# A float32 encoder block on one core: a fifth seven-product unit in ten FFN blocks, fourth sums added by the transfer, residual rows kept in DRAM

## The chip, the cores and the metric

The kernel runs on one core of a Trainium2 chip. The metric is the device time of one execution in microseconds (us), lower is better. Times of several runs are given by their median.

## The reference, cut to what matters

One layer of an encoder with 256 tokens, width 2048 and FFN width 5632, all in float32. Three token mixers (dilated windows, grouped-query attention, cross-attention into 256 memory tokens) are merged by gates; the change lies in what comes after:

```python
x = x + merged @ w_o                                  # residual add, 2048 -> 2048
hf = rms_norm(x, g_ffn) @ w_ffn_in                    # 2048 -> 2 x 5632
x = x + (silu(hf[..., :D_FF]) * hf[..., D_FF:]) @ w_ffn_out   # 5632 -> 2048
```

## The kernel before

**Products.** Every float32 product is made of three fp32r matmuls. A weight block `[128, 2 k-tiles, 512 columns]` (512 KB) is split into a high part `whi` (written by ACT, line 433) and a low part `wlo` (written by VectorE, line 443: the block less `whi`). The tokens' side is kept split in the same way. One product is `x_hi w_hi + x_hi w_lo + x_lo w_hi` for 128 tokens, 128 k and 512 columns, issued at line 79 in this order of terms.

**Blocks and units.** `pair()` computes two 512-column tiles for the two halves of the tokens (four PSUM banks) out of units of k. A plain unit (`D6`, `d6`: the two column tiles of k pair 6) takes eight products of two k-tiles each by two token halves. Units 0 to 3 are taken two and two (`doubles`) by a scheme with seven products for eight, named by the letters X, W, P, Y, Q, Z and H. It needs sums of weight blocks and of tokens: for one double, with blocks b11, b12, b21 and b22, `t = b11 + b12` for W, for P `t` with b22 added (line 576, in its place), for Q this `t` less b11 (line 578, in the place of b11) and for H `t` plus b21 (line 580, in the place of b21). The first sum, `t`, is made by a transfer: b12 is loaded, and a DMA of POOL's queue adds b11 to it (line 530). The others are VectorE additions of 1024 columns. The sums of tokens (`forms`) are made once in `token_sums` from the transposed tiles.

**Order.** The strings `STEPS_...` give the order of steps in a block: `l0` begins double 0 (loads and the accumulating transfer), `r0` loads its second half, `X0` is the product X of double 0, and a dot takes a step of the block before, whose last plain units (third string) run in the front of the next. TensorE's instructions and the loads of SP's queue are kept in the order written. On VectorE and ACT, the instructions that pass through `follow` (`whi`, `wlo`, the sums) keep their order among themselves; the others (the residual adds, the transposed copies) are placed by a scheduler, in a list that the engine then works off in order. Weight blocks are loaded ahead into eleven places (`raw`, `more`, `both`), each free again when the `whi` and `wlo` of its block are written. There are five pairs of `whi` and `wlo`, and `run(everything(), 4)` readies four units ahead.

**Stages.** `merging`, then `projecting` (the product with w_o in two `pair()` calls, residual add into the rows `x`, line 947), then `feeding`: eleven FFN blocks of 512 hidden columns in chunks of 4, 4 and 3, each chunk followed by two parts of the output product (`pairs`), whose result is scaled by a row factor and added to `x` on VectorE (line 1007); in the last chunk each piece of `x` is then stored to the output. The two tiles `x` lie in SBUF from `projecting` to the end.

Of the kernel before, what the change touches and what calls it, by code (L numbers as in the profile page):

```python
# [103 lines left out]
def encoder_block(ctx: ExitStack, tc: tile.TileContext, a: dict, out: bass.AP):  # L104
# [192 lines left out]

    def transposed(src, dst, g=None, lag=1, also=None):


        full = None
        for h in range(2):
            if h:
                yield lag
            tp = bank("tp", "tp")
            for k in range(2):
                for t in range(T):
                    nc.tensor.transpose(tp[:, k * S + t * P:k * S + (t + 1) * P],
                                        src[t][:, (2 * h + k) * P:(2 * h + k + 1) * P], ident)
            if g is None:  # L310
                d = dst(2 * h, 2)
                split(d[0], d[1], tp.rearrange("p (k s) -> p k s", s=S))
            else:
                for k in range(2):
                    d = dst(2 * h + k, 1)
                    split(d[0], d[1], tp[:, k * S:(k + 1) * S], g(2 * h + k))
            if also is not None:
                if full is None:
                    full = s4([P, 2, 4, P], "ffull")
                to, of = full[:, :, 2 * h:2 * h + 2], tp.rearrange("p (k t s) -> p k t s", t=T, s=P)  # L320
                if g is None:
                    nc.scalar.activation(to, of, AF.Copy)
                else:
                    for k in range(2):
                        nc.scalar.activation(to[:, k], of[:, k], AF.Copy, scale=g(2 * h + k))
        if also is not None:
            token_sums(full, also)

    def token_sums(full, to):


        raw = s4([P, 2, 4, P], "fraw")
# [40 lines left out]
    def hold(n, steps):  # L373
        yield n
        yield from steps
# [44 lines left out]
    def halves(*srcs, each=None):  # L420

        count[0] += 1
        pool, n = (more[0], 1) if more and count[0] % 5 == 0 else (wp, 4)
        hi = pool.tile([P, PK, NC], F32R, name="whi", bufs=n)
        lo = pool.tile([P, PK, NC], F32R, name="wlo", bufs=n)
        n = 0
        for v in srcs:
            v = v.unsqueeze(1) if len(v.shape) == 2 else v
            o = slice(n, n + v.shape[1])
            if each:  # L430
                low(0)
                each(n)
            nc.follow(nc.scalar.activation(hi[:, o], v, AF.Copy))  # L433
            due.append((lo[:, o], v, hi[:, o].bitcast(F32)))
            n += v.shape[1]
        return hi, lo
# [3 lines left out]
    def low(n):  # L440

        while len(due) > n:
            nc.follow(nc.vector.tensor_sub(*due.pop(0)))  # L443

    def pair(src, lhs, lists, done, doubles=(), forms=None, operand=None, fresh="", early=False, by_halves=False):

# [10 lines left out]
        nd, wholes = len(doubles), {c: sum(o[0] == c for o in order) for c in "dD"}  # L457
        left = {"Y": 2 * nd + 2 * wholes["d"], "X": 6 * nd, "V": 2 * nd + 2 * wholes["d"],
                "W": 4 * nd + 2 * wholes["D"], "Q": 2 * wholes["D"]}
        if not early:  # L460
            left["X"] += left.pop("V")
        ends = "YV" if early else "YX", "WQ"
        stops = {"X": [left["X"] - n * nd for n in (2, 4, 6)], "W": [left["W"] - 2 * nd]}
        ps, raws, seen, ended = {}, {}, {}, set()
# [76 lines left out]
        def phase_end(kind, hi):  # L541
            seen[kind] = seen.get(kind, 0) + 1
            if seen[kind] < nd:
                return
            with tc.high_priority():
# [13 lines left out]
                if kind == "Q":  # L559
                    new("Q")  # L560
                    wake("Q", hi)
                    nc.follow(nc.vector.tensor_sub(ps["Q"], raws["m5"], ps["X"]))

        def seventh(kind, m):
            of = {"X": "b11", "W": "t", "Y": "b21", "P": "t", "Z": "b22", "Q": "b11", "H": "b21"}[kind]
            bk = {"P": "X", "Q": "X", "H": ends[0][1], "Z": "W"}.get(kind, kind)
            needs = {"Y": "X", "P": "X", "Z": "P", "Q": "P", "H": "Q"}

            def ready():
                r = raws[m]  # L570
                raw = r[of]
                if kind in "PQH" and last_kind[0] == {"P": "W", "Q": "X", "H": "Y"}[kind] + str(m):
                    low(0)
                last_kind[0] = kind + str(m)
                if kind == "P":
                    nc.follow(nc.vector.tensor_add(raw, raw, r["b22"]))
                elif kind == "Q":
                    nc.follow(nc.vector.tensor_sub(raw, r["t"], raw))  # L578
# [3 lines left out]
                for n in {"Q": ["b11"], "Z": ["b22"], "H": ["t", "b21"]}.get(kind, ()):  # L582
                    release(r.pop(n))

                def products():
                    assert kind not in needs or seen.get(needs[kind], 0) == nd, (kind, seen)
                    assert kind != "Z" or seen["W"] == nd
                    for i in range(2):
# [3 lines left out]
                              "Z": lambda: forms(m, i, 2), "Q": lambda: forms(m, i, 3)}[kind]()  # L592
                        mul(bk, st, hi[:, i], lo[:, i])
                    phase_end(kind, hi)
# [4 lines left out]
        def step(o):  # L599
# [3 lines left out]
            if kind in "dD":  # L603
                return whole(n, "dD".index(kind))
            if kind in "lr":
                return lambda: (begin if kind == "l" else begin2)(n)
            return seventh(kind, n)
# [260 lines left out]
    home = lambda n: big if n == 3 else tail  # L868
    mT, x1T, x, room = {}, [], [], []
    ss1 = const.tile([P, T, 4], F32, name="ss1")  # L870
# [55 lines left out]
    def projecting():  # L926
# [8 lines left out]
        ended = []  # L935

        def root():
            yield 4
# [4 lines left out]
        for n in (0, 2):  # L943
            def add(c, r, n=n):
                xc = [x[t][:, (n + c) * NC:(n + c + 1) * NC] for t in range(T)]
                for t in range(T):
                    nc.vector.tensor_add(xc[t], r[t], xc[t])
                ended.append(n + c)
                last = len(ended) == 4

                def later():
# [7 lines left out]
                    if not x1T:  # L959
                        x1T.extend(s8([P, 2, 4, S], "x1T") for _ in range(4))  # L960
                        room.extend(form_room(3))
                    yield from transposed(xc, lambda k, m: (x1T[n + c][:, 0, k], x1T[n + c][:, 1, k]),
                                          lambda k: gT[:, 2, 4 * (n + c) + k:4 * (n + c) + k + 1], 2,
                                          also=room[2 + n + c] if n == 0 else None)
                start(urgent(later()))
# [3 lines left out]
    def store(t, o):  # L969
        nc.sync.dma_start(out=out[t * P:(t + 1) * P, o], in_=x[t][:, o])  # L970
        yield 1

    def feeding():
        for c0, c1 in ((0, 4), (4, 8), (8, KF // 4)):
# [3 lines left out]
            for n in range(c0, c1):  # L978
                av = []

                def hidden(c, v, av=av, n=n - c0, hT=hT):
# [8 lines left out]
                    def later():  # L990
# [5 lines left out]
                    start(urgent(later()))  # L996
                yield pair(lambda u, c, n=n: a["w_ffn"][n][2 * u + 1 - c], x1l, STEPS_FFN if n else STEPS_FFN0, hidden,
                           TWO, by_room(lambda: room[2:]))
            pairs = (STEPS_LAST, STEPS_LAST2) if last else (STEPS_FFN, STEPS_FFN)
            for n in (0, 2):  # L1000
                def output(c, r, n=n, last=last):
                    final = last and n == 2 and c == 0
                    w = NC // 2 if final else NC
                    for t in range(T):
                        for h in range(NC // w):
# [3 lines left out]
                                                           op0=ALU.mult, op1=ALU.add)  # L1009
                            if last:  # L1010
                                start(hold(1 if n else 4, store(t, o)))

# [93 lines left out]
```

## Time and profile before

| | us |
|---|---|
| three runs | 1359.69, 1359.86, 1361.61 |
| median | 1359.86 |
| the profiled execution | 1359.78 |
| its span | 1358.0 |

Between span and time of the profiled execution lie 1.78 us. The clock granted to TensorE was 1.00 throughout. The window from 581 to 700 us holds the end of `projecting` and the first FFN block, the one from 700 to 1281.85 the other ten FFN blocks with the output parts of the first two chunks and the beginning of the last, the one from 1281.85 to the end the last parts. In rows of the profile `mmX`, `mmY`, `mmW` and `mmQ` are the PSUM tiles of a block; a row of the chain of waits gives start, length, engine, tile, line and the number of instructions. A timeline's row gives start and length, and in brackets the idle time ahead of it and who ended that.

### The profile page before, as it was taken

The numbers are of one execution on the slowest core, as the hardware profiler recorded it, in microseconds if no ns is written. First come the engines' busy times: TensorE is split into PE (matmuls) and PEld (weight loads), VectorE is DVE, ScalarE is ACT, GpSimd is POOL, SyncE is SP. The second block draws the span as 40 slices with busy tenths as digits, with TensorE's granted clock in tenths as the row PEclk, the third lists the DMA queues.
The fourth block names the chain that finished last, engine by engine and source line by source line (L and its number), as shares of the span: only waits on it lengthen the run. The fifth ranks groups of instructions, "written<-read, shape, count | busy, mean of one in ns | idle before, by whom it ended". The sixth has DMA issues, their size and how long they took to land.

```text
span 1358.0 us, 17334 instructions
## 1 busy us (share of the span) xinstructions
PE 1351.8 (100%) x6176; PEld 1121.4 (83%) x6176; DVE 1157.1 (85%) x1412; ACT 856.4 (63%) x1112; POOL 53.1 (4%) x60
## 2 busy tenths in 40 slices
PE   9999999999999999999999999999999999999998
PEld 8888888888888888888888888888888888888887
DVE  6878877778879869778899998988999889989997
ACT  7877656656656656657676666555666655566664
POOL 0010000000000000000000000000000000000000
PEclk9999999999999999999999999999999999999999
DMA  9976445556787584785577766688666787666872
GB/s 365 348 231 208 153 146 174 165 171 215 231 264 219 188 293 167 249 279 175 167 232 263 210 208 215 220 263 262 192 218 212 248 263 205 215 230 209 277 221 101
DMA packets 86342, 301.18 MB, mean 222 GB/s; under 512 B 9776, under 2 KB 12336, under 8 KB 86000
## 3 DMA queue, kind: packets, MB, share of 16 engines
q1 hardware_dynamic: 79488, 275.94, 58.1%
q0 software_dynamic: 6624, 24.12, 9.4%
q8 instruction: 48, 0.79, 0.2%
q14 instruction: 38, 0.31, 0.1%
q10 hardware_dynamic: 144, 0.02, 0.0%
HBM read 297.17 MB, written 2.88 MB: 221 GB/s over the span
## 4 chain that ended last, share of the span: by engine, by line
PE 94%; DVE 3%; DMA 1%; issue 1%; ACT 1%; SPq 0%; DVEq 0%; ACTq 0%
PE mmX L79 28%; PE mmW L79 20%; PE mm L79 16%; PE mmY L79 15%; PE mmQ L79 11%; DVE wlo L443 2%; PE tp L79 1%; PE sc L79 1%; PE o L79 1%; DMA raw<-in_w_br 1%; ACT whi L433 1%; PE pT L79 1%; PE hT L79 0%; DMA raw<-in_w_mem 0%; DVE raw L578 0%
## 5 line engine op out<-in xcount | busy, mean ns | idle before, releaser
L433 ACT ACTIVATE whi<-raw 128x1024 fp32r<-128x1024 f32 (+1 forms) x363 | 376.8, 1054 | 235.4 <-PE mmQ L79 53.7
L443 DVE TENSOR_TENSOR wlo<-raw,whi 128x1024 fp32r<-128x1024 f32 (+1 forms) x363 | 437.8, 1220 | 87.9 <-ACT whi L433 82.5
L79 PE MATMUL mm<-whi,xT 128*128 128x512 f32 x640 | 202.3, 393 | 0.0
L433 ACT ACTIVATE whi<-both 128x1024 fp32r<-128x1024 f32 x101 | 106.5, 1055 | 59.0 <-DVE both L578 18.1
L79 PEld LDWEIGHTS mm<-whi,xT 128*128 128x128 f32 x640 | 119.2, 188 | 23.5 <-issue 0.4
L133 DVE TENSOR_TENSOR wlo<-raw,whi 128x1024 fp32r<-128x1024 f32 x82 | 103.3, 1262 | 36.8 <-ACT whi L132 34.3
L443 DVE TENSOR_TENSOR wlo<-both,whi 128x1024 fp32r<-128x1024 f32 x101 | 123.2, 1222 | 11.6 <-ACT whi L433 10.8
L443 DVE TENSOR_TENSOR wlo<-more,whi 128x1024 fp32r<-128x1024 f32 x89 | 108.7, 1222 | 20.9 <-ACT whi L433 19.5
L433 ACT ACTIVATE whi<-more 128x1024 fp32r<-128x1024 f32 x89 | 93.9, 1058 | 50.5 <-PE mmQ L79 15.8
L79 PE MATMUL mm<-wlo,xT 128*128 128x512 f32 x320 | 125.6, 393 | 0.0
L132 ACT ACTIVATE whi<-raw 128x1024 fp32r<-128x1024 f32 x82 | 86.8, 1062 | 56.4 <-PE mm L79 40.3
L79 PE MATMUL mmW<-whi,forms 128*128 128x512 f32 x368 | 122.1, 391 | 0.0
L79 PE MATMUL mmX<-whi,forms 128*128 128x512 f32 x368 | 122.1, 390 | 0.0
L79 PE MATMUL mmX<-whi,x1T 128*128 128x512 f32 x352 | 120.9, 389 | 0.0
L79 PE MATMUL mmY<-whi,x1T 128*128 128x512 f32 x264 | 89.1, 389 | 0.0
L79 PEld LDWEIGHTS mmW<-whi,forms 128*128 128x128 f32 x368 | 69.1, 188 | 14.3
L79 PEld LDWEIGHTS mmX<-whi,forms 128*128 128x128 f32 x368 | 69.1, 188 | 14.3
L79 PEld LDWEIGHTS mmX<-whi,x1T 128*128 128x128 f32 x352 | 66.1, 188 | 13.7
L79 PE MATMUL mmX<-wlo,forms 128*128 128x512 f32 x184 | 71.6, 389 | 0.0
L79 PE MATMUL mmW<-wlo,forms 128*128 128x512 f32 x184 | 71.6, 389 | 0.0
L79 PEld LDWEIGHTS mm<-wlo,xT 128*128 128x128 f32 x320 | 60.2, 188 | 12.4 <-issue 0.7
L79 PE MATMUL mmX<-wlo,x1T 128*128 128x512 f32 x176 | 68.5, 389 | 0.0
(277 smaller groups left out, 2595.2 us busy)
## 6 DMA issues: line engine op xcount, KB each, us to landing
raw<-in_w_ffn SPq DMA_DIRECT2D x116, 512.0 KB, 6.0
raw<-in_w_gate SPq DMA_DIRECT2D x66, 512.0 KB, 4.8
raw<-in_w_qkv SPq DMA_DIRECT2D x64, 512.0 KB, 4.4
raw<-in_w_ffn_out SPq DMA_DIRECT2D x54, 512.0 KB, 6.6
both<-in_w_ffn SPq DMA_DIRECT2D x33, 512.0 KB, 6.4
more<-in_w_ffn SPq DMA_DIRECT2D x27, 512.0 KB, 6.3
raw<-in_w_o SPq DMA_DIRECT2D x22, 512.0 KB, 4.7
both<-in_w_ffn_out SPq DMA_DIRECT2D x20, 512.0 KB, 5.5
```

What stands on the lines that cost most here:

```text
L79: ins = op(*args, **kw)
L132: nc.scalar.activation(hi, src, AF.Copy)
L133: nc.vector.tensor_sub(lo, src, hi.bitcast(F32))
L433: nc.follow(nc.scalar.activation(hi[:, o], v, AF.Copy))
L443: nc.follow(nc.vector.tensor_sub(*due.pop(0)))
```

## The change

In ten of the eleven FFN blocks (all but the first) `STEPS_FFN5` replaces `STEPS_FFN`. The plain unit 6 (`D6`, `d6`) becomes a seven-product unit within one k pair: its four blocks of one k-tile by 512 columns play b11, b12, b21 and b22. It runs in four parts, `S1` (products X and W), `S2` (P, Y), `S3` (Q, Z) and `S4` (H). Its `t` is the loaded pair of k-tiles with half a block added by a transfer of 256 KB (`s0`, line 560); its other sums are VectorE additions of 512 columns (lines 577, 579, 581). The sums of 128 tokens that it needs, `lone`, are made once in `projecting` from k-tiles 12 and 13.

In the same blocks H's sum is no longer added on VectorE: `a0` and `a1` add b21 to `t` by an accumulating DMA on POOL's queue (line 554), after Q has read `t`; b21 itself is loaded later, at Y.

The rows `x` after the residual add of `projecting` are stored to a DRAM tile `held` on SP's queue (8 stores of 256 KB, `keep`). In the first two chunks ACT writes the scaled output of a part to `o`, and a DMA on POOL's queue adds it to `held` (line 1096, 8 of 512 KB). `rows_back` loads the rows again for the last chunk. The 2 MB of SBUF that `x` gave up hold two more `both` tiles, four places, from the second FFN block on. Lines of the kernel after: `whi` is written at about line 444, `wlo` at 455, the sums of the doubles are at 644, 646 and 648, the subtractions at the ends of P and Q at 618 and 622 (558 and 562 before), the residual add at 1023, the gate product at 1076 (988 before), the accumulating transfer of `t` at 545.

VectorE at the end of w_o's product and the beginning of the first FFN block, before. `x0`, `x1` are the two halves of the residual rows, `mmY_5743` and `mmX_5736` the last banks of w_o's product; the `wlo` here belong to the first FFN block, in the order in which TensorE uses them:

```order
L443 TENSOR_TENSOR wlo_6221<-both_3324,whi_6220 128x1024
L578 TENSOR_TENSOR more0_6035<-raw0_6033,more0_6035 128x1024
L443 TENSOR_TENSOR wlo_6238<-both_3324,whi_6237 128x1024
L558 TENSOR_TENSOR mmW_6173<-m5_6218,mmX_6118 128x512
L443 TENSOR_TENSOR wlo_6249<-more0_6035,whi_6248 128x1024
L947 TENSOR_TENSOR x0_5579<-mmY_5743,x0_5579 128x512
L443 TENSOR_TENSOR wlo_6260<-raw4_6127,whi_6259 128x1024
L947 TENSOR_TENSOR x1_5598<-mmX_5736,x1_5598 128x512
L443 TENSOR_TENSOR wlo_6281<-raw1_6088,whi_6280 128x1024
```

The same place after (`fraw` and `lone` are the new token sums):

```order
L342 TENSOR_TENSOR fraw_6191<-ffull_6188 128x256
L138 SCALAR_TENSOR_TENSOR x1T_5799<-tp_6228,gT_82,x1T_5799 128x256
L343 TENSOR_TENSOR fraw_6191<-fraw_6191,ffull_6188 128x128
L344 TENSOR_TENSOR fraw_6191<-fraw_6191,ffull_6188 128x128
L1023 TENSOR_TENSOR x0_5580<-mmY_5744,x0_5580 128x512
L135 TENSOR_TENSOR lone_5803<-fraw_6191,lone_5803 128x512
L1023 TENSOR_TENSOR x1_5599<-mmX_5737,x1_5599 128x512
L455 TENSOR_TENSOR wlo_6238<-both_3324,whi_6237 128x1024
L646 TENSOR_TENSOR more0_6041<-raw0_6039,more0_6041 128x1024
L455 TENSOR_TENSOR wlo_6255<-both_3324,whi_6254 128x1024
L618 TENSOR_TENSOR mmW_6172<-m5_6226,mmX_6124 128x512
L455 TENSOR_TENSOR wlo_6266<-more0_6041,whi_6265 128x1024
```

The three `wlo` that stood ahead of the first residual add (6221, 6238 and 6249, now 6238, 6255 and 6266) stand behind the second one, with the sum and the subtraction between them.

POOL's queue over two FFN blocks, before: one `l` transfer for each double.

```order
L530 DMA raw6_8090<-in_w_ffn 128x1024
L530 DMA raw0_8095<-in_w_ffn 128x1024
L530 DMA more0_8408<-in_w_ffn 128x1024
L530 DMA more1_8413<-in_w_ffn 128x1024
```

And after, from the `l0` of one block to the `s0` of the second next (545 is `l`, 554 is `a`, 560 is `s`):

```order
L545 DMA raw0_8863<-in_w_ffn 128x1024
L554 DMA both_6432<-in_w_ffn 128x1024
L545 DMA both_6433<-in_w_ffn 128x1024
L554 DMA raw6_8511<-in_w_ffn 128x1024
L560 DMA both_6433<-in_w_ffn 128x512
L545 DMA both_6432<-in_w_ffn 128x1024
L554 DMA raw0_8863<-in_w_ffn 128x1024
L545 DMA raw6_9221<-in_w_ffn 128x1024
L554 DMA both_6433<-in_w_ffn 128x1024
L560 DMA more1_9226<-in_w_ffn 128x512
```

Each block's `a0` and `a1` stand between and behind the `l0` and `l1` of the block after it.

VectorE in the first part of the last chunk's output, before (`raw4` is read for Z1, `raw2` for H0, `both` for H1):

```order
L580 TENSOR_TENSOR raw2_11137<-more0_11082,raw2_11137 128x1024
L443 TENSOR_TENSOR wlo_11316<-raw4_11171,whi_11315 128x1024
L133 TENSOR_TENSOR hT_11304<-tp_11325,hT_11304 128x512
L562 TENSOR_TENSOR mmQ_11343<-m5_11245,mmX_11164 128x512
L580 TENSOR_TENSOR both_3324<-more1_11087,both_3324 128x1024
L443 TENSOR_TENSOR wlo_11334<-raw2_11137,whi_11333 128x1024
L133 TENSOR_TENSOR hT_11304<-tp_11356,hT_11304 128x512
L443 TENSOR_TENSOR wlo_11347<-both_3324,whi_11346 128x1024
```

And after (`wlo_11470` is Z1's, 11488 H0's, 11501 H1's):

```order
L648 TENSOR_TENSOR both_6432<-both_6433,both_6432 128x1024
L135 TENSOR_TENSOR hT_11429<-tp_11452,hT_11429 128x512
L455 TENSOR_TENSOR wlo_11470<-raw1_11332,whi_11469 128x1024
L135 TENSOR_TENSOR hT_11429<-tp_11479,hT_11429 128x512
L622 TENSOR_TENSOR mmQ_11497<-m5_11408,mmX_11325 128x512
L648 TENSOR_TENSOR both_3324<-both_3324 128x1024
L455 TENSOR_TENSOR wlo_11488<-both_6432,whi_11487 128x1024
L455 TENSOR_TENSOR wlo_11501<-both_3324,whi_11500 128x1024
```

Both `hT` writes now stand ahead of H0's `wlo`, where one stood behind it.

The diff, cut to its core:

```diff
+STEPS_FFN5 = ("l0 l1 s0 X0 X1 . W0 W1 S1 r0 P0 . r1 P1 S2 Y0 Y1 . Q0 a0 Q1 a1 S3",
+              "Z0 Z1 D4 H0 D5 H1 D7 S4", "d4 d5 d7")
...
-    def transposed(src, dst, g=None, lag=1, also=None):
+    def transposed(src, dst, g=None, lag=1, also=None, single=None):
...
+            if single is not None and h == 0:
+                one, of = s4([P, 1, 4, P], "ffull"), tp.rearrange("p (k s) -> p k s", s=S)
+                for k in range(2):
+                    nc.scalar.activation(one[:, 0, 2 * k:2 * k + 2].rearrange("p t s -> p (t s)"), of[:, k], AF.Copy,
+                                         scale=g(k) if g else 1.0)
+                token_sums(one, single)
...
         def begin2(m):
             j = doubles[m][1]
-            raws[m].update({"b22": load((src(j, 1),), 0, PK), "b21": load((src(j, 0),), 0, PK)})
+            raws[m]["b22"] = load((src(j, 1),), 0, PK)
+            if m not in added:
+                raws[m]["b21"] = load((src(j, 0),), 0, PK)
+
+        def fourth(m):
+            nc.gpsimd.dma_start(out=raws[m]["t"].rearrange("p k n -> p (k n)"), in_=src(doubles[m][1], 0),
+                                accum_op=ALU.add)
+
+        def begin_single(_):
+            t = load((src(single[0], 1),), 0, PK)
+            raws["s"] = {"t": t, "b1": load((src(single[0], 0),), 0, PK)}
+            nc.gpsimd.dma_start(out=t[:, 0], in_=src(single[0], 0)[:, :NC], accum_op=ALU.add)
...
+        def part(n):
+            kinds = ("XW", "PY", "QZ", "H")[n - 1]
...
+                if n == 2:
+                    nc.follow(nc.vector.tensor_add(t[:, 0], t[:, 0], t[:, 1]))
+                elif n == 3:
+                    nc.follow(nc.vector.tensor_sub(b1[:, 0], t[:, 0], b1[:, 0]))
+                elif n == 4:
+                    nc.follow(nc.vector.tensor_add(b1[:, 1], t[:, 0], b1[:, 1]))
+                hi, lo = halves(*((b1[:, 0], t[:, 0]), (t[:, 0], b1[:, 1]), (b1[:, 0], t[:, 1]), (b1[:, 1],))[n - 1])
...
+                if kind == "Y" and m in added:
+                    r["b21"] = load((src(doubles[m][1], 0),), 0, PK)
...
-                elif kind == "H":
+                elif kind == "H" and m not in added:
                     nc.follow(nc.vector.tensor_add(raw, r["t"], raw))
...
+        def keep(i, xc):
+            for t in range(T):
+                nc.sync.dma_start(out=held[:, t, i * NC:(i + 1) * NC], in_=xc[t])
+            yield 1
...
                     nc.vector.tensor_add(xc[t], r[t], xc[t])
+                start(hold(3, keep(n + c, xc)))
...
+                if n == 1:
+                    more_room = [s8([P, 2, PK, NC], "both", F32) for _ in range(2)]
+                    free.extend((Part(r[:, i]), f"more_room{i}") for r in more_room for i in range(2))
...
+            if last:
+                start(hold(8, rows_back()))
             for n in (0, 2):
                 def output(c, r, n=n, last=last):
+                    if not last:
+                        o = s4([P, T, NC], "o")
+                        for t in range(T):
+                            nc.scalar.activation(o[:, t], r[t], AF.Copy, scale=r_f[:, 0, t:t + 1])
+                        nc.gpsimd.dma_start(out=held[:, :, (n + c) * NC:(n + c + 1) * NC], in_=o, accum_op=ALU.add)
+                        return
```

More of the change, by code (lines that the diff above doesn't have):

```diff
@@ L329, in token_sums @@
     def token_sums(full, to):
[L332 removed]
+        n = full.shape[1]
+        raw = s4([P, n, 4, P], "fraw")
         nc.vector.tensor_sub(raw[:, :, :2], full[:, :, :2], full[:, :, 1::2])
@@ L426, in halves @@
         n = 0
+        due.append([])
         for v in srcs:
@@ L442, in low, with pair @@
         while len(due) > n:
-            nc.follow(nc.vector.tensor_sub(*due.pop(0)))
-    def pair(src, lhs, lists, done, doubles=(), forms=None, operand=None, fresh="", early=False, by_halves=False):
+            for part in due.pop(0):
+                nc.follow(nc.vector.tensor_sub(*part))
+    def pair(src, lhs, lists, done, doubles=(), forms=None, operand=None, fresh="", early=False, by_halves=False, single=None):
         lists = [l.split() for l in lists]
@@ L462, in pair @@
         ends = "YV" if early else "YX", "WQ"
-        stops = {"X": [left["X"] - n * nd for n in (2, 4, 6)], "W": [left["W"] - 2 * nd]}
+        stops = {"X": [left["X"] - n * units for n in (1, 2, 3)], "W": [left["W"] - units]}
         ps, raws, seen, ended = {}, {}, {}, set()
@@ L604, in step @@
                 return whole(n, "dD".index(kind))
-            if kind in "lr":
-                return lambda: (begin if kind == "l" else begin2)(n)
+            if kind in "lras":
+                return lambda: {"l": begin, "r": begin2, "a": fourth, "s": begin_single}[kind](n)
+            if kind == "S":
+                return part(n)
             return seventh(kind, n)
@@ L868, in encoder_block @@
     home = lambda n: big if n == 3 else tail
-    mT, x1T, x, room = {}, [], [], []
+    held = dram.tile([P, T, D], F32, name="held")
+    mT, x1T, x, room, lone = {}, [], [], [], []
     ss1 = const.tile([P, T, 4], F32, name="ss1")
@@ L971, in store, with rows_back @@
         yield 1
+    def rows_back():
+        x[:] = [s8([P, D], f"xb{t}", F32) for t in range(T)]
+        for t in range(T):
+            nc.sync.dma_start(out=x[t], in_=held[:, t])
+            yield 1
     def feeding():
```

63 lines of the change are left out of this document (47 added, 16 removed).

## The prediction

> **What bounds the kernel now.** I read the page first (totals, queues, chain by engine), then the windows by stage, then the chain and VectorE's timeline at the two places where the change alters VectorE's order.
>
> ```profile
> span 1358.0 us, 17334 instructions
> PE 1351.8 (100%) x6176; PEld 1121.4 (83%) x6176; DVE 1157.1 (85%) x1412; ACT 856.4 (63%) x1112; POOL 53.1 (4%) x60
> q1 hardware_dynamic: 79488, 275.94, 58.1%
> q0 software_dynamic: 6624, 24.12, 9.4%
> PE 94%; DVE 3%; DMA 1%; issue 1%; ACT 1%; SPq 0%; DVEq 0%; ACTq 0%
> L433 ACT ACTIVATE whi<-raw 128x1024 fp32r<-128x1024 f32 (+1 forms) x363 | 376.8, 1054 | 235.4 <-PE mmQ L79 53.7
> ```
>
> TensorE carries 94% of the chain. The windows below (columns: window, length, busy time of PE, PEld, DVE, ACT, POOL, then clock, DMA share, GB/s) are w_o's end with the first FFN block, the ten later FFN blocks with the first FFN-out parts, two regular FFN blocks, and the last parts.
>
> ```profile
> 581.00:700.00 119.00, 119.00 (x547) 98.23 (x546) 101.41 (x126) 76.69 (x107) 4.32 (x5) 1.00 0.68 218
> 700.00:1281.85 581.85, 581.85 (x2606) 481.67 (x2605) 524.99 (x501) 365.83 (x396) 24.19 (x28) 1.00 0.71 229
> 991.42:1033.18 41.76, 41.76 (x189) 34.56 (x189) 38.70 (x39) 27.68 (x31) 1.75 (x2) 1.00 0.70 231
> 1033.18:1074.95 41.77, 41.77 (x190) 34.58 (x189) 37.45 (x36) 26.12 (x28) 1.72 (x2) 1.00 0.70 228
> 1281.85:1358.00 76.15, 72.03 (x327) 59.36 (x325) 66.57 (x67) 40.85 (x44) 1.74 (x2) 1.00 0.52 163
> ```
>
> From 581 to 1282 TensorE never rests, at full clock. So a matmul taken away there is time gained, and a stall put there is time lost; before 581 the instructions stand in the same order. Behind TensorE comes VectorE with 37.5 to 38.7 of 41.8 us: 3 to 4 us of room in a block.
>
> ```profile
> 1033.18 2.72 PE mmX L79 x12
> ...
> 1046.79 4.08 PE mmY L79 x18
> ```
>
> Both rows give 0.2267 us a matmul, six (one product of a pair of weight tiles) in 1.36.
>
> **The change, part by part.** *Matmuls.* In each of ten blocks a unit of eight plain products becomes one of seven: 3 matmuls fewer. 10 x 3 x 0.2267 = 6.80 us less, all of it on the path.
>
> *VectorE at the end of w_o.* This is what I think decides the case. The order of VectorE (shown with the change) now has the two residual adds `x0<-mmY`, `x1<-mmX` ahead of three `wlo` that stood before them. VectorE's timeline of before there:
>
> ```profile
> 658.30 0.68 DVE L947 TENSOR_TENSOR x<-mmQ,x 128x512 f32<-128x512 f32 x1
> ...
> 672.10 1.23 DVE L443 TENSOR_TENSOR wlo<-both,whi 128x1024 fp32r<-128x1024 f32 x1
> 673.24 1.23 DVE L578 TENSOR_TENSOR more<-raw,more 128x1024 f32<-128x1024 f32 x1
> 674.37 1.23 DVE L443 TENSOR_TENSOR wlo<-both,whi 128x1024 fp32r<-128x1024 f32 x1
> 675.51 0.70 DVE L558 TENSOR_TENSOR mmW<-m,mmX 128x512 f32<-128x512 f32 x1
> 676.10 1.23 DVE L443 TENSOR_TENSOR wlo<-more,whi 128x1024 fp32r<-128x1024 f32 x1
> 677.24 0.69 DVE L947 TENSOR_TENSOR x<-mmY,x 128x512 f32<-128x512 f32 x1
> 677.84 1.23 DVE L443 TENSOR_TENSOR wlo<-raw,whi 128x1024 fp32r<-128x1024 f32 x1
> 678.97 0.69 DVE L947 TENSOR_TENSOR x<-mmX,x 128x512 f32<-128x512 f32 x1
> 679.57 1.23 DVE L443 TENSOR_TENSOR wlo<-raw,whi 128x1024 fp32r<-128x1024 f32 x1
> ...
> 682.70 0.70 DVE L562 TENSOR_TENSOR mmQ<-m,mmX 128x512 f32<-128x512 f32 x1 [0.55 <-PE mmX L79]
> ...
> 690.12 1.22 DVE L443 TENSOR_TENSOR wlo<-raw,whi 128x1024 fp32r<-128x1024 f32 x1
> ```
>
> Start to start, 1024 columns take 1.135 us and 512 take 0.60. TensorE's chain at the same place:
>
> ```profile
> 675.38 1.36 PE mmY L79 x6
> 676.75 1.36 PE mmX L79 x6
> 678.11 1.36 PE mmY L79 x6
> 679.47 1.37 PE mmX L79 x6
> 680.83 0.44 PE tp L79 x4
> ...
> 691.31 1.51 PE mmW L79 x6
> ```
>
> The first two rows are w_o's last product; the third is the first FFN block's, with the `wlo` of 672.10. The add of `mmX` cannot start before 678.11. It then ends its turn at 678.11 + 0.04 + 0.60 = 678.75, and only then comes the `wlo` that TensorE wants at 678.34 (its first matmul takes `whi`): it ends at 679.97, 1.6 late. The add of line 646 and the next `wlo` end at 678.75 + 3 x 1.135 + 0.09 = 682.24; TensorE, resumed at 679.97, wants it at 681.33: 0.9 more. The mmW subtraction and a third `wlo` end at 683.97, wanted at 683.60: 0.4. That is 2.9 us. VectorE is then still behind. At the x1 add's end it owes five 1024-column operations and one of 512 that were done by 679.57 before, 5 x 1.135 + 0.60 = 6.28 us, and from there to the end of the `wlo` of 690.12 (691.26) it had 11.69 us, some 0.85 of it idle (0.55 at 682.70, the rest as a wait for `whi` near 680.8, an estimate from the spacing). 678.75 + 6.28 + 10.84 + 0.09 = 695.96. Before, that `wlo` arrived just as wanted (mmW took 1.51 for 1.36 at 691.31); with 2.9 of delay it is wanted at about 694.3: another 1.7. Sum 4.6 us. The new 128-token sums (`lone`) fall in VectorE's wait for the adds and cost nothing; without that wait they would add some 1.3 us (an estimate from 0.60 for 512 columns). Bounds: 0, if VectorE finds the slack that I miss, and 6.3, all that is owed.
>
> *VectorE and ACT in the ten blocks.* VectorE loses two adds and two `wlo` of 1024, and gains three adds and seven half `wlo` of 512: 10 x 0.60 - 4 x 1.135 = +1.46 us, so 38.9 to 40.2 of 41.1. ACT exchanges two `whi` of 1.054 for seven of about 0.6 (half, plus a start): +2.1 on 27.7. Cost 0 under TensorE; the cover is what VectorE runs ahead, and it shrinks. In the two early output parts the scaled outputs go from VectorE to ACT, 16 operations, both hidden.
>
> *The fourth sums (`a0`, `a1`).* These have the nearest due time. Rows for the transfers (all of the accumulating kind from 700 to 1320, then two issues, a plain load's median, and a `wlo` that stands two units behind its use):
>
> ```profile
> L530 POOL DMA_DIRECT2D more<-in_w_ffn x8: 862/862/883, 767.6 to 1184.8; - x8
> DMA to landing us min/median/max: 6.1/9.0/11.3
> ```
>
> ```profile
> 1100.17 0.86 POOL L530 DMA_DIRECT2D more<-in_w_ffn_out  x1 [39.61 <-DVE wlo L443]
> 1102.54 0.86 POOL L530 DMA_DIRECT2D more<-in_w_ffn_out  x1 [1.51 <-DVE wlo L443]
> ```
>
> ```profile
> both<-in_w_ffn SPq DMA_DIRECT2D x28, 512.0 KB, 6.3
> ```
>
> ```profile
> 1045.84 1.22 DVE L443 TENSOR_TENSOR wlo<-raw,whi 128x1024 fp32r<-128x1024 f32 x1
> ```
>
> `a1` may start when Q1's subtraction is done and its `t` free. On POOL it stands behind the next block's `l1`, whose plain load gets its place one `wlo` ahead of Q0's subtraction, 4.0 us (three of 1.135 and 0.60) before Q1's. With 6.3 for the load and 0.86 for the issue, `a1` is issued 3.2 us after the subtraction and, with the longest landing of a pair (11.3), lands at 14.5. It is wanted at: one `wlo`, S3's add and Q1's `wlo` (2.87), the lead of VectorE over TensorE, taken as 2.45 (the `wlo` of 1045.84 ends at 1047.06 and is wanted at 1046.79 + 2 x 1.36 = 1049.51), TensorE's way to H1 (Q1, S3, Z0, Z1, H0 at 1.36, D4 and D5 at 2.72, two groups of transposes at 0.44: 13.1), less `whi` and `wlo` (2.3): 16.1. So 1.6 us are left. `a0` has 14.6 by the same working (one more VectorE operation, 2.72 less of TensorE's way) and needs no more than 0.86 + 11.3. Bounds: 0, and beyond that the time by which `a1` is late, ten times. I take 0.5 in all, near the lower bound, since each number but the lead is a late one.
>
> The Trainium skill, "DMA: Bandwidth & Descriptors", section Queues, rings and completion order, says that a DMA engine goes round the queues it has work for, packet by packet. By that rule accumulations keep their turn when loads crowd, and the sum stays as above; a queue that served loads first would add to every `a1`. The 11.3 at 0.70 of the engines is no test of a fuller queue.
>
> *Stores on SP's queue, and the engines.* SP waits with each store of residual rows for its adds, and the loads behind wait too. The add of 658.30 ends at 658.98; a w_o load held by it lands 6.3 later and its `whi` ends at 666.3. From there to the x0 add VectorE has six operations of 1.135 and seven small ones, 2.3 us: 675.4, and the add cannot start before 676.75. The cover is VectorE's wait that I priced above; a load later by over 1.3 us would lengthen that stall. The load held by the add that ends at 678.75 is wanted eight operations later. The engines: q1 cost 0.581 x 1358.0 / 275.94 = 2.86 us a MB, q0 5.3, thus 1.5 and 2.8 us for 512 KB. A block had 16 loads and 2 accumulations, 29.6 of 41.8 (0.71, as in the windows); now 16 and 4.5: 36.6 of 41.1, 0.89. Eight accumulations into DRAM (2.8 each by the same price, no row shows one) and the residual's stores and reads come once each; the four new places let loads start earlier. Taken as 0, at most 1 us.
>
> *The last parts.* In the first of them a second `hT` write now stands ahead of H0's `wlo`, the first row here; its use is the third.
>
> ```profile
> 1308.03 1.23 DVE L443 TENSOR_TENSOR wlo<-raw,whi 128x1024 fp32r<-128x1024 f32 x1
> 1309.17 0.69 DVE L133 TENSOR_TENSOR hT<-tp,hT 128x512 fp32r<-128x512 f32 x1
> ```
>
> ```profile
> 1310.02 2.72 PE mmX L79 x12
> ```
>
> That `wlo` ended 1.0 us before its use (1309.26 against 1310.25); 0.60 moved ahead leaves 0.4. Taken as 0.2, between 0 and 0.6.
>
> **Sum.** 1359.78 (profiled execution, 0.08 under the median 1359.86) - 6.80 + 4.6 + 0.5 + 0.2 = 1358.3 us.
>
> **The rivals.** *The gain comes whole or nearly.* 1359.78 - 6.80 + 0.2 = 1353.2 without a stall at w_o's end, up to 1357.1 with most of one. For it: only one place is altered so, and VectorE has room on either side. Against it: VectorE's list runs in order, and the rows above leave it no lead there.
>
> *Slower: `a1` becomes the bound.* Place: H1 in every block of the new kind. It decides when `a1` lands over 16.1 us after Q1's subtraction, thus when the load or the two transfers take 1.6 us longer at 0.89 of the engines than at 0.70. Each us beyond costs up to 10. Half a microsecond to one: 1363 to 1368. Against it: before, no accumulation in these rows took over 11.3.
>
> *Slower: POOL's descriptor writing stops VectorE.* 2.5 more issues a block of 0.86 are 2.15 us; VectorE would have 37.45 + 1.46 + 2.15 = 41.06 to 42.31 against 41.09, up to 1.2 a block: 1358 to 1370, middle 1364. Against it: the issues above took 862 to 883 ns, with VectorE at nine tenths. The Trainium skill, "SBUF — State Buffer", section on who interferes with whom, has a rule of this kind: a VectorE instruction with two SBUF inputs contends with a GpSimd instruction that reads SBUF. The even 862 speaks against it here.
>
> *The new unit saves nothing*, if its halves split matmuls further: the instruction order shows 21 where 24 stood, so this has no chance of its own.
>
> **How the numbers follow.** About 0.2% (2.7 us: 1357.1 and 1362.6) is what a measurement can tell from no change. The forecast's own case (1357 to 1360.5) has 0.50, a fifth of it below 1357.1; the whole gain 0.22; `a1` late 0.22, a tenth of it under 1362.6; POOL against VectorE 0.06. Faster 0.22 + 0.10 = 0.32; same 0.40 + 0.02 = 0.42; slower 0.26. The range 1354.6 to 1364.5 leaves out the lower third of the whole gain (0.07) and the upper half of the slower cases (0.12).
>
> **What would show it.** Right: the windows of ten blocks at 41.1 us, TensorE full; near 678 to 695 TensorE idle for 4 to 5 us behind `wlo` of line 455, and VectorE idle 3 us ahead of line 1023; DMA share near 0.89; accumulations of line 554 landing in under 12. Wrong: no gap there, or gaps in the FFN blocks that end with line 455 after a wait for line 554's transfer.

## The result, and the profile after

The changed kernel took 1397.76 us (median of four runs, 1397.58 to 1398.87), the kernel before 1359.78 beside it: ratio 1.0278, 95% interval 1.026 to 1.0296. It is 38 us slower, where the prediction said 1358.3 and at most 1364.5.

The page of the kernel after, the lines that answer to those of before:

```profile
span 1395.9 us, 17542 instructions
PE 1361.7 (98%) x6146; PEld 1121.9 (80%) x6146; DVE 1161.0 (83%) x1460; ACT 885.1 (63%) x1181; POOL 88.2 (6%) x98
q1 hardware_dynamic: 80928, 280.14, 55.9%
q0 software_dynamic: 13120, 41.42, 16.2%
```

The 30 matmuls are gone (6146 for 6176). Yet TensorE's busy time rose by 9.9 us, where 6.8 less were due: 16.7 us too much. Its idle time (span less busy) rose from 6.2 to 34.2. 28.0 + 16.7 - 6.8 = 37.9, the difference of the spans. The mean granted clock of this execution was 0.990; the missing hundredth of its span is some 14 of the 16.7 us (an estimate), and the rest was not followed up. What TensorE waited for (us in total, times, longest), after:

```profile
PE mmX L81 <- ACT mmY L613: 23.9, 10, 5.0
PE mmX L81 <- DVE mmW L618: 1.5, 1, 1.5
PE idle L81 <- POOL ident masks.py:199: 1.4, 1, 1.4
PE mmY L81 <- DVE wlo L455: 1.2, 1, 1.2
PE mmW L81 <- DVE wlo L455: 0.9, 3, 0.3
PE mmX L81 <- DVE wlo L455: 0.7, 1, 0.7
```

Ten waits, one for each new block, stand on an instruction that the prediction does not mention: ACT's copy of `mmX` into `mmY` (line 613; 553 before), made when the products X are complete. P accumulates into the same `mmX`, so P0 must not start before the copy has read it. One block's ACT, then TensorE at the same place:

```profile
980.10 1.06 ACT L444 ACTIVATE whi<-raw 128x1024 fp32r<-128x1024 f32 x1 [1.56 <-PE mmW L81]
981.83 0.63 ACT L444 ACTIVATE whi<-both 128x512 fp32r<-128x512 f32 x1 [0.68 <-DVE both L577]
982.37 0.61 ACT L444 ACTIVATE whi<-raw 128x512 fp32r<-128x512 f32 x1
982.89 0.58 ACT L613 ACTIVATE mmY<-mmX 128x512 f32<-128x512 f32 x1
983.41 0.58 ACT L616 ACTIVATE m<-mmW 128x512 f32<-128x512 f32 x1
```

```profile
980.34 0.39 PE L81 MATMUL mmX<-whi,x1T 128*128 128x512 f32 x1
980.56 0.39 PE L81 MATMUL mmW<-whi,lone 128*128 128x512 f32 x1
...
981.02 0.39 PE L81 MATMUL mmW<-whi,lone 128*128 128x512 f32 x1
983.52 0.50 PE L81 MATMUL mmX<-whi,forms 128*128 128x512 f32 x1 [2.12 <-ACT mmY L613]
```

The last matmul of X begins at 980.34. Behind it TensorE has only S1's own W product, three matmuls (0.68 us), and then P0. Before, X1 ended X, and a plain unit, W0 and W1 (5.4 us) stood between it and P0. There the last matmul of X, the copy and the first of P0 were:

```profile
1035.52 0.39 PE L79 MATMUL mmX<-whi,x1T 128*128 128x512 f32 x1
1036.22 0.58 ACT L553 ACTIVATE mmY<-mmX 128x512 f32<-128x512 f32 x1
1041.18 0.39 PE L79 MATMUL mmX<-whi,forms 128*128 128x512 f32 x1
```

So the copy was done 4.4 us before P0. After the change ACT, in order, first writes the `whi` of P1 (it waits for TensorE to free a buffer) and of S2's two halves (they wait for a sum), and comes to the copy at 982.89. The granted clock in that stretch, in windows of 2 us, stands in the column before the DMA share:

```profile
979.00:981.00 2.00, 2.00 (x10) 1.67 (x9) 2.00 (x2) 0.90 (x1) 0.00 (x0) 1.00 0.50 201
981.00:983.00 2.00, 0.41 (x2) 0.00 (x0) 2.00 (x4) 1.32 (x4) 0.00 (x0) 1.00 0.29 55
983.00:985.00 2.00, 1.48 (x5) 1.25 (x6) 1.10 (x3) 1.93 (x3) 0.00 (x0) 0.83 0.55 219
985.00:987.00 2.00, 2.00 (x6) 1.52 (x6) 1.23 (x2) 1.06 (x1) 0.88 (x1) 0.50 0.01 2
987.00:989.00 2.00, 2.00 (x9) 1.59 (x8) 2.00 (x2) 0.00 (x0) 0.00 (x0) 0.82 1.04 133
```

After the gap the clock is 0.83, 0.50 and 0.82 in three windows: at half for some 3.4 us, which costs 1.7 us of TensorE's work (estimates from these windows). Such a fall followed seven of the eight gaps of 2.12 us and more in the new blocks, and neither of the two of 1.66.

Near 678 to 695, where the prediction put a stall of 4.6 us, TensorE has gaps of 1.25, 1.53 and 0.32 us. VectorE after:

```profile
675.79 0.69 DVE L1023 TENSOR_TENSOR x<-mmY,x 128x512 f32<-128x512 f32 x1 [0.67 <-PE mmY L81]
676.40 0.68 DVE L135 TENSOR_TENSOR lone<-fraw,lone 128x512 fp32r<-128x512 f32 x1
677.15 0.69 DVE L1023 TENSOR_TENSOR x<-mmX,x 128x512 f32<-128x512 f32 x1
677.76 1.22 DVE L455 TENSOR_TENSOR wlo<-both,whi 128x1024 fp32r<-128x1024 f32 x1
```

### The profile page after: what moved, and what is told of

Its sections match the earlier page's. It is cut to its first block, busy times and chain, and to the rows that moved or that the text cites. A ratio compares the mean times of both kernels' runs of the same rounds, so it can differ in the third digit from the quotient of the medians.

```text
span 1395.9 us, 17542 instructions
## 1 busy us (share of the span) xinstructions
PE 1361.7 (98%) x6146; PEld 1121.9 (80%) x6146; DVE 1161.0 (83%) x1460; ACT 885.1 (63%) x1181; POOL 88.2 (6%) x98
## 5 line engine op out<-in xcount | busy, mean ns | idle before, releaser
L444 ACT ACTIVATE whi<-raw 128x1024 fp32r<-128x1024 f32 (+1 forms) x320 | 316.3, 1000 | 200.3 <-PE mmQ L81 37.5
L455 DVE TENSOR_TENSOR wlo<-raw,whi 128x1024 fp32r<-128x1024 f32 (+1 forms) x320 | 364.7, 1150 | 86.8 <-ACT whi L444 84.2
L444 ACT ACTIVATE whi<-both 128x1024 fp32r<-128x1024 f32 (+1 forms) x195 | 194.5, 1006 | 118.6 <-DVE both L644 24.1
L455 DVE TENSOR_TENSOR wlo<-both,whi 128x1024 fp32r<-128x1024 f32 (+1 forms) x195 | 224.6, 1158 | 44.6 <-ACT whi L444 43.2
L81 PE MATMUL mmX<-whi,forms 128*128 128x512 f32 x368 | 129.6, 407 | 25.4 <-ACT mmY L613 23.9
L455 DVE TENSOR_TENSOR wlo<-more,whi 128x1024 fp32r<-128x1024 f32 (+1 forms) x88 | 103.6, 1178 | 23.7 <-ACT whi L444 22.9
L444 ACT ACTIVATE whi<-more 128x1024 fp32r<-128x1024 f32 (+1 forms) x88 | 89.8, 1022 | 43.6 <-PE mmQ L81 8.3
L81 PEld LDWEIGHTS mmX<-whi,forms 128*128 128x128 f32 x368 | 71.3, 194 | 45.1 <-ACT mmY L613 28.1
L81 PE MATMUL mmY<-whi,x1T 128*128 128x512 f32 x244 | 85.5, 407 | 0.2 <-ACT whi L444 0.2
```

Of the source, the lines that this page charges most:

```text
L81: ins = op(*args, **kw)
L455: nc.follow(nc.vector.tensor_sub(*part))
```

## The experiments

All were timed beside the kernel before, whose median lay between 1359.45 and 1359.73 in the four groups of runs. The table has medians in us. Its rows say where S1 and the copy stand, its columns whether `a0` and `a1` stand behind the next block's `l0` and `l1` on POOL's queue, ahead of them, or are left out (H's sums on VectorE again). The other runs follow in the text.

| | a behind l | a ahead of l | no a |
|---|---|---|---|
| S1 behind W1 | 1397.8 (the change) | 1393.6 `a_first` | 1405.0 `no_a` |
| S1 ahead of W0 | 1400.4 `s1_first` | 1368.7 `a_first_s1` | 1378.4 `s1_first_no_a` |
| S1 behind W1, copy two units earlier on ACT | 1396.1 `copy_free` | 1369.5 `a_first_copy_free` | |
| unit 6 plain | 1381.4 `plain6_a` | | 1364.4 `plain6` |

### First: is it the copy?

```diff
 s1_first
-STEPS_FFN5 = ("l0 l1 s0 X0 X1 . W0 W1 S1 r0 P0 . ...
+STEPS_FFN5 = ("l0 l1 s0 X0 X1 . S1 W0 W1 r0 P0 . ...
 s1_between
+STEPS_FFN5 = ("l0 l1 s0 X0 X1 . W0 S1 W1 r0 P0 . ...
 copy_free
-                    nc.follow(nc.scalar.activation(ps["Y"], ps["X"], AF.Copy))
+                    nc.scalar.activation(ps["Y"], ps["X"], AF.Copy)
```

> S1 moved ahead of W0 and W1 in the ten blocks, nothing else. Theory (copy): P0 waits for ACT's copy mmY<-mmX because only S1's own W product (0.68 us) lies between the end of X and P0, and the gap of 2 us or more then halves the clock for some microseconds. With W0 and W1 behind S1 (0.68 + 2.72 us of cover) the ten gaps go, and the slow clock with them: 1397.8 - 23.9 - about 15 = 1357 to 1361. Rival (transfers): the fuller DMA engines make the weights late, and the copy is only where it shows; then TensorE waits for wlo or whi instead, and the time stays above 1375.

> S1 moved between W0 and W1. Theory (copy): cover of 0.68 + 1.36 us in place of 0.68, and the copy stands behind one unit's whi less on ACT: gaps of 0 to 0.8 us in place of 1.7 to 2.5, too short for the clock to fall: 1358 to 1367. Rival (transfers): no change, above 1390. Were the clock to fall for another reason than the gaps, 16 us of it would stay: above 1373.

> The order of steps as in the changed kernel; only the copy mmY<-mmX is no longer chained behind the whi's on ACT, and stands two units earlier in ACT's list (ahead of the whi of P1 and of S2's halves). Theory (copy's place in ACT's list): gaps shrink to about the copy itself less the cover, 0 to 1 us, clock full: 1358 to 1368. Rival (the cover alone decides, ACT's list does not matter): gaps of over 1.5 us stay, above 1385. Rival (transfers): above 1375.

They took 1400.36 (ratio 1.0294, 1.0264 to 1.0323), 1397.05 (1.0271, 1.0248 to 1.0294) and 1396.14 (1.0274, 1.0257 to 1.0291). The copy's waits fell from 23.9 us to 0, 10.6 and 2.1, and the time by at most 1.6 us: the numbers of the rival, that transfers are late. In `s1_first` TensorE waits for `wlo` and `whi` instead, and behind them ACT waits for transfers. The largest sums of ACT's waits there between 700 and 1320 us:

```profile
ACT whi L444 <- DMA both<-in_w_ffn: 38.7, 10, 9.0
ACT whi L444 <- DVE raw L646: 26.9, 16, 2.2
ACT whi L444 <- DMA raw<-in_w_ffn: 21.2, 5, 7.5
```

One block of `s1_first`: Q1's subtraction on VectorE, POOL's queue, and ACT and VectorE at H1, each a row of a timeline:

```profile
773.12 1.22 DVE L646 TENSOR_TENSOR raw<-both,raw 128x1024 f32<-128x1024 f32 x1
```

```profile
771.92 0.86 POOL L554 DMA_DIRECT2D both<-in_w_ffn  x1 [2.39 <-DVE both L646]
779.05 0.86 POOL L545 DMA_DIRECT2D more<-in_w_ffn  x1 [6.27 <-DMA more<-in_w_ffn]
779.59 1.21 POOL L554 DMA_DIRECT2D both<-in_w_ffn  x1
```

```profile
790.80 1.06 ACT L444 ACTIVATE whi<-both 128x1024 fp32r<-128x1024 f32 x1 [7.07 <-DMA both<-in_w_ffn]
```

```profile
791.89 1.23 DVE L455 TENSOR_TENSOR wlo<-both,whi 128x1024 fp32r<-128x1024 f32 x1 [5.41 <-ACT whi L444]
```

`a1` (779.59) could have gone at 774.34, when the subtraction ended. It stood behind `l1` of the next block (779.05), which waited for its plain load. It landed some 16.4 us after the subtraction. That is the prediction's rival, at its place.

```diff
 plain6
-... STEPS_FFN5 if n else STEPS_FFN0, hidden,
+... STEPS_FFN if n else STEPS_FFN0, hidden,
```

> Unit 6 plain in the ten blocks and H's sums on VectorE (the old order of steps); rows in DRAM, the four places, the lone sums and the accumulating outputs stay. Theory: no copy gaps, no slow clock, no matmuls saved; what is left is the stall at w_o's end (3.1 us measured) and 0.7 in the last part: 1362 to 1366. If the rows in DRAM or the new places cost much by themselves: above 1368.

It took 1364.37 (1.0039, 1.0025 to 1.0052), as expected: what stays beside the ten blocks' new unit and sums costs 4.6 us.

### Second: the accumulations and the copy, one by one

```diff
 a_first_s1 (with the order of s1_first); the same for line 545 and line 560
-            nc.gpsimd.dma_start(out=raws[m]["t"]..., in_=src(doubles[m][1], 0), accum_op=ALU.add)
+            nc.follow(nc.gpsimd.dma_start(out=raws[m]["t"]..., in_=src(doubles[m][1], 0), accum_op=ALU.add))
 s1_first_no_a
+STEPS_FFN5 = ("l0 l1 s0 X0 X1 . S1 W0 W1 r0 P0 . r1 P1 S2 Y0 Y1 . Q0 Q1 S3", ...
 no_a
+STEPS_FFN5 = ("l0 l1 s0 X0 X1 . W0 W1 S1 r0 P0 . r1 P1 S2 Y0 Y1 . Q0 Q1 S3", ...
 plain6_a
+STEPS_FFN5 = ("l0 l1 X0 X1 . r0 W0 r1 W1 P0 P1 . Y0 Y1 . Q0 a0 Q1 a1 .",
+              "Z0 Z1 D4 H0 D5 H1 D6 D7", "d4 d5 d6 d7")
```

> On POOL's queue a0 and a1 of a block now stand ahead of l0 and l1 of the next (with S1 ahead of W0 and W1 as in s1_first). The traces of the first runs show ACT's whi of H0 or H1 waiting for the accumulating transfer up to 9.0 us, and a1 issued 5 us after its subtraction because l1's load had not landed. Theory (a1 late through its place on POOL's queue): issued at once, it lands about 11 us after the subtraction, ahead of its use: 1356 to 1363. Rival (the queue's rate: too many accumulations for the engines, whatever the order): l' or s' come late instead, and the time stays above 1375.

> H's sums on VectorE again (no a0, a1), the seven-product unit kept, S1 ahead of W0 and W1. Theory (late accumulations): the waits for DMA go; VectorE carries 2.27 us more a block, 41.2 to 42.5 for 41.1: 1356 to 1368, with short waits for wlo. Rival (the seven-product unit itself, its halves and its transfer, costs the time): above 1375.

> As the changed kernel, but H's sums on VectorE (no a0, a1); S1 stays behind W1. Theory (late accumulations): ACT no longer falls behind, so the copy mmY<-mmX comes at most 1 us late: 1358 to 1372. Rival (S1's place and its short cover are a loss of their own): gaps of 2 us with a slow clock in each block: above 1385.

> Unit 6 plain (no S steps), but H's sums by a0 and a1, at the same places as in the changed kernel. Beside plain6 (1364.4) it has the accumulations alone. Theory (late accumulations, by themselves): above 1372, with whi waiting for them. Rival (they are late only together with the new unit, by VectorE's load or by s0's transfers): 1360 to 1368.

`a_first_s1` took 1368.68 (1.0064, 1.0047 to 1.0081), 31.7 less than `s1_first` by the order of the transfers on POOL's queue alone, though still above the theory's 1356 to 1363. The same block there, POOL:

```profile
772.26 0.86 POOL L554 DMA_DIRECT2D both<-in_w_ffn  x1 [24.96 <-DVE both L646]
775.27 0.86 POOL L554 DMA_DIRECT2D both<-in_w_ffn  x1 [2.16 <-issue]
775.81 1.21 POOL L545 DMA_DIRECT2D both<-in_w_ffn  x1
```

The transfers of line 554 (`a0`, `a1`): who waited for them, and the time from issue to landing, in `s1_first` and then in `a_first_s1`:

```profile
  ACT whi L444: 63.4, 16
DMA to landing us min/median/max: 7.1/10.5/13.2
```

```profile
  ACT whi L444: 9.6, 8
DMA to landing us min/median/max: 7.1/8.3/10.7
```

`no_a` took 1404.95 (1.033, 1.0311 to 1.0348): against the theory and for its rival, S1's place is a loss of its own. With no fourth sums by transfer at all, the copy's waits are longer than in the change:

```profile
PE mmX L81 <- ACT mmY L613: 28.4, 10, 5.0
PE mmX L81 <- DVE mmW L618: 2.5, 2, 1.6
```

`s1_first_no_a`, with neither loss, took 1378.38 (1.013, 1.0111 to 1.0149), the number of the rival, that the new unit itself costs the time. In its trace VectorE's list is too long: in the two blocks from 987.63 to 1072.69 VectorE was busy for 84.1 of 85.1 us, 42.1 a block, where TensorE was to need 41.1. TensorE waits in short pieces for `wlo`, and ACT no more than 4.5 us at once for a transfer:

```profile
PE mmX L81 <- DVE wlo L455: 5.1, 8, 0.8
PE mmW L81 <- DVE wlo L455: 4.8, 8, 0.8
```

`plain6_a` took 1381.44 (1.0164, 1.0148 to 1.018), the theory's number: the accumulations alone, behind `l`, cost 17 us over `plain6`, also without the new unit.

> The fourth corner: S1 behind W1 as in the changed kernel, but a0 and a1 ahead of the next block's l0 and l1 on POOL's queue. So far: both as changed 1397.8, S1 early alone 1400.4, both moved 1368.7, and without a0 and a1 1405 with S1 late. Theory (two losses that cover each other, the copy behind ACT's list and the late accumulation): the copy gaps of 2 to 3 us stay in each block, with the slow clock behind them: 1392 to 1406. Rival (the late accumulation is the one cause, and S1's place matters only as a shift of it): 1365 to 1380.

`a_first` (the same edit, S1 behind W1) took 1393.61 (1.0251, 1.0237 to 1.0265), the theory's number. What the copy cost there:

```profile
PE mmX L81 <- ACT mmY L613: 21.1, 10, 2.8
```

So there are two losses, and each covers the other: with the late copy TensorE stands still for 2 us a block, in which `a1` lands (ACT waited 31.3 us for line 554's transfers in the change, for 63.4 in `s1_first`); with `a1` late ACT and VectorE are behind, and an early copy has nothing to feed. Moving one alone changed the time by +3 and by -4 us, both together by -29.

### Third: list or cover, the clock, and what is left

```diff
 a_first_copy_free: a_first, and the edit of copy_free
 a_first_wake: a_first, and ahead of the copy (ns is 1 in the ten blocks, else 0)
+                    for _ in range(6 * ns):
+                        nc.tensor.matmul(ps["Y"], lhsT=hi[:, 0, :P], rhs=hi[:, 0], start=True, stop=True)
```

> a_first with the copy mmY<-mmX no longer chained behind the whi's, two units earlier in ACT's list; S1 stays behind W1. Theory (the copy's place in ACT's list): it comes within about a microsecond of X's end, gaps of 0 to 0.7 us, clock full: 1365 to 1373, as with S1 moved (1368.7). Rival (0.68 us of cover is too little for any copy): gaps of 1.5 us or more: above 1380.

It took 1369.46 (1.0071, 1.0055 to 1.0086), as expected: 24.2 us less than `a_first` by the copy's place in ACT's list alone, with S1 where the change has it. Its 0.68 us of cover are not the trouble, but for the first new block, where a gap of 2.07 us stayed:

```profile
PE mmX L81 <- ACT mmY L613: 2.7, 3, 2.1
```

> a_first (1393.6, gaps of 1.7 to 2.8 us in each of ten blocks) with six more matmuls of 0.2267 us, whose result is overwritten, put into TensorE's list ahead of S1's W product in each block: 1.36 us that would have been idle. The copy is late anyway, so P0 starts when it did. Theory (the clock falls after an idle time of some 2 us): the clock stays at 1.00 and the slow matmuls (some 13 us) go: 1379 to 1384. Rival (the clock falls for another reason, or falls seldom enough not to matter): 1391 to 1396.

It took 1387.40 (1.0195, 1.0178 to 1.0212), 6.2 below `a_first`, between the two readings. The same 4 us of a block, `a_first` and then `a_first_wake`, in windows:

```profile
1026.00:1028.00 2.00, 1.59 (x5) 1.31 (x6) 1.10 (x3) 1.82 (x3) 0.00 (x0) 0.75 0.45 182
1028.00:1030.00 2.00, 2.00 (x7) 1.51 (x6) 1.07 (x1) 1.05 (x1) 0.00 (x0) 0.50 0.00 0
```

```profile
1026.00:1028.00 2.00, 2.00 (x10) 1.62 (x9) 1.39 (x2) 1.48 (x2) 0.00 (x0) 1.00 0.00 0
1028.00:1030.00 2.00, 2.00 (x11) 1.65 (x10) 2.00 (x2) 0.52 (x1) 0.00 (x0) 1.00 0.54 145
```

Gaps of 2.12 us became 0.76, and the clock stays at 1.00 behind them: it does follow the idleness. From gap to gap a block took 43.5 us for 45.1, thus 1.6 less. Six such stretches became 1.5 to 1.6 us shorter, 9.5 in all. The sum is less than the 13 expected, since behind the other gaps (two of some 1.66 us, one of 2.28) the clock of `a_first` had not fallen, and in the first new block the gap stayed at 3.03 us, with a slow clock behind it.

```diff
 a_first_s1_x, plain6_x: as a_first_s1 and plain6, and
-                    nc.vector.tensor_add(xc[t], r[t], xc[t])
+                    nc.follow(nc.vector.tensor_add(xc[t], r[t], xc[t]))
 a_first_s1_x_hold, plain6_x_hold: as those, and
-                start(hold(3, keep(n + c, xc)))
+                start(hold(14, keep(n + c, xc)))
```

> a_first_s1 with the residual adds chained into VectorE's list where they are written, so that they stand behind the three wlo again, as before the change. Theory (order at w_o's end): the gaps of 2.9 us near 678 to 682 go, 0 to 2 us of other small waits may grow: 1364 to 1367 for 1368.7. Rival (VectorE is so full there that the stall only moves): 1368 to 1370.

> As a_first_s1_x, and each store of residual rows to DRAM is issued 14 ticks after its add rather than 3, so that SP's queue does not wait for the add with loads behind it. Theory (held loads crowd into the first new block): the gaps near 711 to 715 (3.0 us) go: 1361 to 1365. Rival (the four new places and the table load make the crowd): no change to a_first_s1_x.

> plain6 (unit 6 plain, no a0, a1) with the residual adds behind the three wlo as before the change. Theory: the stall at w_o's end (3.4 us of gaps in plain6) goes, and with it nearly all of its 4.6 us: 1359.5 to 1361.5, so rows in DRAM and four more places cost about nothing by themselves. Rival (rows in DRAM cost the 4.6): 1363 to 1365.

> plain6_x (1364.2) with the stores of residual rows issued 14 ticks after their adds. Theory (SP's queue, waiting for the adds, holds the loads behind them and VectorE starts late): the gaps of 2.5 us near 679 to 694 go: 1360.5 to 1362. Rival (the token sums and rows cost it elsewhere): 1363.5 to 1365.

With the residual adds behind the three `wlo` as before, `a_first_s1_x` took 1366.87 for 1368.68 (within the theory's range, but the intervals of the two overlap) and `plain6_x` 1364.15 for 1364.37, the rival's number. A gap of 1.54 us before Q0 of the first FFN block stayed in both. SP's queue still waited for the adds, with loads behind its stores. In `plain6_x`, between 640 and 720 us (sum, times, longest):

```profile
SPq L81 <- DVE x L1023: 35.4, 4, 22.8
```

With the stores to DRAM issued later as well, `a_first_s1_x_hold` took 1365.91 (1.0046, 1.0033 to 1.0058), short of its theory: of the stall near 678 to 695 a gap of 0.27 us is left, but three of together 2.1 us stand near 710 to 714. `plain6_x_hold` took 1360.74 (1.0008, 0.9999 to 1.0017), the theory's number, and no such row is among SP's waits. It says that rows in DRAM, four more places and token sums cost no time that can be told, once SP's queue does not wait for the adds.

No version with the new unit beats the kernel before. With both losses undone a regular block still takes 42.27 us (`a_first_s1`, 1026.57 to 1068.84) for 41.77 before and 41.1 in the prediction: TensorE is busy for 41.40 of it and waits 0.87 us for a `wlo`, though VectorE is busy for 39.81 only. That wait was not followed further.

## Why the prediction was wrong, point by point

**Matmuls.** There are 30 fewer, as said. That their 6.80 us were "all of it on the path" held only while nothing new stood on it.

**VectorE and ACT in the ten blocks, "Cost 0 under TensorE".** This is the first of two steps that failed. It counted ACT's busy time (`whi`, 2.1 us more a block) and not the order of ACT's list, in which a copy stands that TensorE waits for. S1 ends both X and W; the copy that had a plain unit, W0 and W1 to cover it was left with 0.68 us, and with the `whi` of P1 and S2 ahead of it. Measured: 23.9 us of gaps, a slow clock behind seven of them, and 24.2 us less once the copy alone was moved (`a_first` to `a_first_copy_free`). VectorE's busy time itself came as forecast (39.8 of 38.9 to 40.2 us in a regular block).

**The clock.** At 1.00 in every window of before, it was taken as given. Some 1.6 us went after most gaps of 2.12 us and more. The Trainium skill, "TensorE: Matmul & The Clock Gate", section HAM oscillation, warns of idle gaps over about 3.4 us; here 2.12 us was enough in most cases (the exceptions are one gap of 2.12 us in the change and one of 2.28 in `a_first`) and 1.66 in none, and the measurement decides.

**`a1`, "0.5 in all".** This is the second step that failed. The rival named the mechanism, the place, H1, and a limit of 16.1 us; it had a chance of 0.22 and 1363 to 1368. Measured in the block above: issued 5.3 us after the subtraction for 3.2, since `l1`'s load took 8.0 us (6.3 taken), and landed after 16.4. By the limit that is 0.3 us late, yet VectorE stood for 5.41 us, and TensorE in three gaps for 1.9. The limit seems wrong in kind: it let the transfer use up VectorE's whole lead at no cost, though VectorE, with 1 to 2 us of room in a block, cannot build it up again before the next block's `a1` (an argument from these numbers; no run tests it by itself). The cost was 31.7 us between `s1_first` and `a_first_s1`, three times the rival's highest price, and 26.7 between `copy_free` and `a_first_copy_free`. In the change itself the copy's gaps hid most of it: 4.2 us came back when `a0` and `a1` alone were moved.

**The turn of the queues.** By the rule that the prediction took from the Trainium skill, "DMA: Bandwidth & Descriptors", section Queues, rings and completion order (a DMA engine goes round its queues packet by packet), accumulations keep their turn. The traces agree, in that accumulations were not starved. Those of line 554 took 7.1 to 13.2 us to land in `s1_first` (5.4 to 13.8 in the change, where under 12 was the forecast; 6.1 to 11.3 before), at 0.82 of the engines from 700 to 1320 us. Issued first they took 7.1 to 10.7 in `a_first_s1`, at 0.85 of the engines from 700 to 1310. So the order of issue, not a lack of turns, made them late.

**End of w_o.** There was a stall at the place, 3.1 us measured for 4.6, but the order of the adds is not shown to be its main cause: putting them back gave 0.2 us in `plain6_x`. VectorE waited 0.67 us ahead of the first add, where 3 us was forecast. The term "Stores on SP's queue", taken as 0, was the wrong one: moving the stores as well gave another 3.4 us. The stores alone were not tried, so the shares stay open. That `plain6` cost just the 4.6 us of the sum is luck.

**The last part.** TensorE waited 0.74 us for H0's `wlo`, for 0.2 and a bound of 0.6.

**POOL against VectorE** did not show. From 700 to 1320 us `wlo` of 1024 columns took 1.22 us on average, before and after. Issues of line 545 took 0.859 to 0.895 us in `s1_first`; those of line 554 took up to 1.23, when they came right behind another issue.

## What to carry to other kernels

When a step is moved, list every instruction that closes an accumulation, on every engine, and what stands ahead of it in that engine's list: work done ahead (here weight splits four units early) sits in front of the copy that TensorE waits for now. A lead is a stock: a wait that uses it up may cost nothing once, but costs each time if the engine behind it has no room to refill it. When two losses cover each other, undoing one alone shows next to nothing; test all four corners.

## What the runs showed of the hardware

A gap of 2.12 us on TensorE was followed in most cases by two or three windows of 2 us at a granted clock of 0.50 to 0.83; gaps of 1.66 us were not. Six matmuls whose result is thrown away, in gaps of 2.12 us, kept the clock at 1.00. An accumulating transfer of 512 KB into SBUF landed 5.0 to 17.9 us after its issue (shortest in `a_first_wake`, longest in `a_first_s1_x`), and a queue that waits for one load delays the next transfer by the whole wait, here by 5 us.
